# A decoder trunk in one kernel: other staging places, another queue and another order in the gate passes of layer A

## The chip, the cores and the metric

The kernel runs on one core of a Trainium2 chip. The metric is device time in microseconds (us) of one execution; a smaller number is better. Beside the times of whole executions there is one profiled execution, with a trace of every instruction. Engines are named as in the profile: PE multiplies matrices, PEld loads its stationary operand, DVE is the vector engine, ACT the scalar engine, POOL is GpSimd, and SP issues most of the data transfers. POOL issues transfers too, on a queue of its own. Each of these engines works its instructions off in the order in which they stand in its own program, and semaphores hold an instruction back until what it needs is there.

## What is computed

A trunk of two decoder layers over 512 tokens of width 2048, in float32. Layer A, in which the change lies, is sparse attention with a gate:

```
proj = x @ w_in
q, k, v, gate, iq, ik, iw = split(proj)          # 16 query heads, 4 key/value groups of 128
q, k = partial_rope(q), partial_rope(k)           # the first 32 of each head's 128 rows turn
iscore = sum_h relu(iq_h . ik) * iw_h * scale     # an index score for each query and key
idx = top_k(iscore, 128)                          # causal; 128 keys for each query
wts = softmax(q . k[idx] / sqrt(128))
o = wts @ v[idx]
h = (o * silu(gate)) @ w_o
x = layer_norm(alpha * x + h); x = x + (p @ w_p) * sigmoid(x @ w_g)
```

Layer B has the same frame around a stick-breaking attention. Every product is made of float32 operands that are split into two parts each, a high and a low one, and is the sum of three matmuls (high by high, high by low, low by high; lines 147 to 149).

## The kernel before

**Weights.** A weight tile comes from memory into a `raw` place (tiles `raw`, or a lent home, which the trace shows as `f` or `t`). ACT writes its high part (`wh` or `sh`), DVE then its low part (`wl` or `sl`); there are three buffers of each of the four names. So each weight costs one ACT and one DVE instruction, and two matmuls in three need it.

**Strassen in four passes.** Keys and values (columns of `w_in`), and then the gates, are computed with seven products in place of eight (m1 to m7). `gemm_quarters` runs a pass: for each of 8 steps along the contraction it takes one weight for each product of the pass and makes 2 x 3 matmuls of 512 columns with it. For the gates the first pass makes m2 and m4 from weights as they come, the second m1 and m7 (m7 from a difference of weights: one more DVE instruction a step), the third m6, m5 and m3 (from sums of weights: three more a step). The pass that follows the gates, called the chunk here, is `gemm_s` with `added_items`: the last quarter of the queries, all seven products at once with matmuls of 256 columns. Its weight sums for units 3 to 7 are prepared by transfers that add on arrival (lines 492 to 494: one on SP's queue, two on POOL's); those of units 0 to 2 by two more DVE instructions each.

**What sets the order.** PE's order is written by hand in the generators. Other work is put between PE's steps: `steps(gemm, n)` lets n PE steps (three matmuls each) be written, `pumped_at(gemm, when)` takes a piece of the queue `bg` at each step listed in `when`, and `paced(...)` pins an instruction to its place in the program. What isn't pinned is placed by a scheduler. On DVE and ACT all of this ends up in one row.

**The pieces in the queue.** `rounds` are the last rounds of the search for the 128 largest index scores: each is a MAX and a MATCH_REPLACE (a read of 8 largest values, and their removal), and the last piece is a mask of two instructions. `rounds[2:]` are two rounds and the mask.

**Keys.** The four key groups are complete before the gates' first pass. Their place `Kf` (the tile F[1], `f` in the trace) is needed for gate squares, so each group is turned (DVE, STREAM_TRANSPOSE in blocks of 32) into one of two halves of the tile `kx` (`stage`), and sent from there to memory (`turned_keys`, `kd` in the trace). The third and fourth group must wait until the first and second have been read out of `kx`. `key_back(g, b)` brings a quarter of a group back: for b = 0 the 32 rows that turn come into the packed tile `KP` (`rp` in the trace), and `key_turns` turns them there (a shuffle, two products, a sum); for b = 1, 2, 3 the others come straight into `Kf` later, in the chunk. Each is one DMA of 64 KB.

**Gate squares.** Inside the chunk, `turn_gate(g, t, rows)` applies SiLU to one half of a gate quarter (ACT), turns it (DVE) into a half of `kx` chosen by `stage(t)`, and `gates_out` sends it to memory (`heldg`). There are eight squares, and two places: the third must wait until the first has been read out, and so on. The gate quarters still have to be summed in between (`add_gates`, one DVE instruction each, with the tiles `u` and `t5` among the summands).

**Evictions at the end of a pass.** Results leave PSUM by ACT or DVE. Of the gates' m1, a copy goes to `u` (ACT) and a sum into c11 (DVE, `f<-f,m`), written behind the second pass; PE needs the banks of m1 again for m3, the third product of the third pass (line 1235: `m6, m5, m3 = pair(1, "m6"), pair(3, "m5"), pair(5, "m3")`, and m1, m7 are `pair(5)`, `pair(7)`).

Of the kernel before, what the change touches and what calls it, by code (L numbers as in the profile page):

```python
# [28 lines left out]
C_Q, C_K, C_V, C_G, C_IQ, C_IK = 0, 2048, 2560, 3072, 5120, 6144  # L29
# [22 lines left out]
def steps(gen, n):  # L52
    for _ in range(n):
        next(gen, None)
# [23 lines left out]
def trunk_kernel(  # L78
# [16 lines left out]
    nc = tc.nc  # L95
# [315 lines left out]
    bg = deque()  # L411

    def paced(fn, *args):
        was, pinned[0] = pinned[0], True
        fn(*args)
        pinned[0] = was
# [9 lines left out]
    def pumped_at(gen, when):  # L426
        for i, _ in enumerate(gen):
            if bg and i in when:
                one()
            yield  # L430
# [8 lines left out]
    def drain():  # L439
        while bg:  # L440
            one()
# [138 lines left out]
    def gemm_quarters(items, products):  # L580

        for k in range(NK // 2):
            for get, outs in products:
                pinned[0] = True
                w = next(items)
                pinned[0] = False
                h, l = get(k)
                for j, out in enumerate(outs):
                    s = slice(j * 128, (j + 1) * 128)
                    mm3(out, (h[:, s], l[:, s]), w, k == 0, k == NK // 2 - 1)  # L590
                    yield
# [268 lines left out]
    turned_keys = [dram.tile([128, 4, 128], F32, name=f"kd{g}") for g in range(4)]  # L860
# [42 lines left out]
    held_g = {g: dram.tile([4, 128, 4, 128], F32, name=f"heldg{g}") for g in (1, 2)}  # L903
# [6 lines left out]
    items = Ahead(all_items(), 2)  # L910
# [75 lines left out]
    gemm = first_pair(two)  # L986
    gemm = pumped_at(gemm, (*(46 + 5 * i // 2 for i in range(28)), *range(120, 128, 2)))
# [102 lines left out]
    gemm = pumped_at(both(), (*range(0, 32, 2), *range(34, 104, 3), *range(104, 128, 2)))  # L1090
# [14 lines left out]
    sp = pc_.enter_context(ss(name="spa", bufs=1, side="right"))  # L1105
    u, t3, t4, t5, kx = (sp.tile([128, 2, T], F32, name=n) for n in ("u", "t3", "t4", "t5", "kx"))
# [14 lines left out]
    def half(row, t):  # L1121
        return lambda k: (XH[k + row][:, t : t + H], XL[k + row][:, t : t + H])

    def summed(i):
        return lambda k: tuple(part[:, k] for part in CA[i])

    gemm = pumped(queries(2, (7, 0, 1, 2)), 3)
# [15 lines left out]
    rounds = [bg.pop() for _ in range(len(bg) - 2)][::-1]  # L1143
    for n, k in zip((0, 1, 2, 3, 5, 6, 8, 9), range(8)):
        bg.insert(n, lambda k=k: split(XH[k][:, H:T], XL[k][:, H:T], T1[1][k]))
    m2, m4 = pair(3, "m2"), pair(5, "m4")
# [8 lines left out]
    m1, m7 = pair(1, "m1"), pair(7, "m7")  # L1155
# [37 lines left out]
    def key_rows(g, rows=slice(0, 128)):  # L1193
        return Kf[rows, :, g * 128 : (g + 1) * 128]

    def stage(n):
        return kx[:, n % 2].rearrange("p (b n) -> p b n", b=4)

    def key_back(g, b):
        src = turned_keys[g].rearrange("(a j) b n -> b j a n", a=4)[b]  # L1200
        fetched = nc.sync.dma_start(key_rows(g, slice(32 * b, 32 * b + 32)) if b else KP[32 * g : 32 * g + 32], src)
        tc.keep_in_program_order(fetched)

    m2, m4 = pair(1, "m2"), pair(3, "m4")
    gemm = pumped_at(gemm_quarters(gates, ((half(8, 0), m2), (summed(2), m4))), (1, 5, 9, 13, 17))
    steps(gemm, 19)
    for g in range(4):
        paced(turn_blocks, stage(g), key_rows(g))
        steps(gemm, 3)
        nc.sync.dma_start(turned_keys[g], stage(g))  # L1210
    run(gemm)
    drain()
    c11, c12, c21, c22 = F[1][:, 0:2], F[3][:, 2:4], F[1][:, 2:4], F[3][:, 0:2]
# [2 lines left out]
    for j in range(2):  # L1216
        paced(lambda: act.activation(c21[:, j], m4[j], AF.Copy, scale=-1.0))
    m1, m7 = pair(5, "m1"), pair(7, "m7")
    bg.extend(rounds[2:])
    key_turns = turned_rows(KP, lambda g: key_rows(g, slice(0, 32)), by_place, by_token)  # L1220
    gemm = pumped_at(gemm_quarters(gates, ((half(0, 0), m1), (summed(1), m7))), range(1, 32, 4))
    steps(gemm, 11)
    for g in range(4):
        key_back(g, 0)
        steps(gemm, 1)
    steps(gemm, 4)
    bg.extend(key_turns[:3])
    run(gemm)
    drain()
# [8 lines left out]
    two = [flat[0][:, 4 * n : 4 * n + 4].rearrange("p a t -> p (a t)") for n in range(2)]  # L1238
    third, fourth = (t.rearrange("p a t -> p (a t)") for t in (t3, t4))
    places = [(two[0], two[1], third, fourth)[n % 4] for n in range(8)]  # L1240
    items = Ahead(added_items(w_in_a, (C_Q + 1536,), places, sp, range(3, 8)), 2)
    paced(items.prime)
    steps(gemm, 2)
    for j in range(2):
# [16 lines left out]

    turned_gates = deque()

    def turn_gate(g, t, rows):
        paced(act.activation, rows, rows, AF.Silu)
        paced(turn_blocks, stage(t), rows.rearrange("p (a n) -> p a n", a=4))
        turned_gates.append((g, t))

    def gates_out():
        g, t = turned_gates.popleft()  # L1270
        tc.keep_in_program_order(nc.sync.dma_start(held_g[g][t], stage(t)))

    steps(gemm, 3)
    turn_gate(1, 0, c11[:, 0])
# [21 lines left out]
    def some_back(n):  # L1296
        for _ in range(n):
            key_back(*backs.pop(0))
            steps(gemm, 2)

    some_back(3)
    add_gates(c12, t5)
    some_back(5)
    add_gates(c12, u)
    some_back(4)
    steps(gemm, 1)
    for g, t, rows in ((2, 2, c22[:, 0]), (2, 3, c22[:, 1]), (1, 2, c12[:, 0])):
        turn_gate(g, t, rows)
        steps(gemm, 7)
        gates_out()  # L1310
    nc.gpsimd.dma_start(F[0][:, 0:2], held_q[0][:, 0:2])
    turn_gate(1, 3, c12[:, 1])
# [1 line left out]
    gates_out()  # L1314
    run(gemm)
    drain()

    nc.gpsimd.dma_start(F[0][:, 2:4], held_q[0][:, 2:4])
    items = Ahead(rest_items(), 2).prime()
# [1269 lines left out]
```

## Time and profile before

| | |
|---|---|
| runs shown | 1815.38, 1813.75, 1807.22 us; median 1813.75 |
| profiled execution | 1807.65 us |
| its span, first to last instruction | 1805.4 us |
| PE busy | 1794.0 us of the span |
| DVE busy | 1534.2 us |
| ACT busy | 1055.1 us |
| POOL busy | 59.3 us |
| gates' first pass on PE | about 307 to 329 us from the span's start |
| gates' second pass | about 329 to 351 us |
| gates' third pass | about 351 to 386 us |
| the chunk | about 386 to 431 us |

A row of the timeline has the start and the duration in us, the engine, the line of the source, the operation, what it writes and reads, and how many like it were merged; in square brackets stands the time for which the engine was idle before it, and what ended that. `L118` is a helper through which every ACT and DVE instruction is recorded, so those are told apart by tiles. A waits row has the engine and line that waited, what ended the wait, the total, how often, and the longest.

### The profile page before, as it was taken

The numbers are of one execution on the slowest core, as the hardware profiler recorded it, in microseconds if no ns is written. First come the engines' busy times: TensorE is split into PE (matmuls) and PEld (weight loads), VectorE is DVE, ScalarE is ACT, GpSimd is POOL, SyncE is SP. The second block draws the span as 40 slices with busy tenths as digits, with TensorE's granted clock in tenths as the row PEclk, the third lists the DMA queues.
The fourth block names the chain that finished last, engine by engine and source line by source line (L and its number), as shares of the span: only waits on it lengthen the run. The fifth ranks groups of instructions, "written<-read, shape, count | busy, mean of one in ns | idle before, by whom it ended". The sixth has DMA issues, their size and how long they took to land. (4 is left out here: it accounts for less than half of the span.)

```text
span 1805.4 us, 26352 instructions
## 1 busy us (share of the span) xinstructions
PE 1794.0 (99%) x9191; PEld 1538.9 (85%) x9191; DVE 1534.2 (85%) x2958; ACT 1055.1 (58%) x1937; POOL 59.3 (3%) x113
## 2 busy tenths in 40 slices
PE   9999999999999999999999999999999999999999
PEld 9888888788888899888888888887788889988898
DVE  7888999898878899976568889978887889997997
ACT  4554355456676544575346554578888854557644
POOL 0001110011030000000000000001000000000000
PEclk9999999999999999999999999999999999999999
DMA  7524477766431344422438777736432244434344
GB/s 219 162 74 151 153 230 233 220 195 195 133 92 47 108 125 128 132 95 96 144 111 264 232 250 238 257 106 158 127 106 71 70 117 129 141 116 144 125 146 123
DMA packets 145780, 269.27 MB, mean 149 GB/s; under 512 B 13232, under 2 KB 57776, under 8 KB 144368
## 3 DMA queue, kind: packets, MB, share of 16 engines
q1 hardware_dynamic: 139728, 250.42, 44.8%
q0 software_dynamic: 5632, 16.78, 3.5%
q8 instruction: 72, 1.18, 0.3%
q14 instruction: 60, 0.49, 0.1%
q10 hardware_dynamic: 288, 0.39, 0.1%
HBM read 239.50 MB, written 23.07 MB: 145 GB/s over the span
## 5 line engine op out<-in xcount | busy, mean ns | idle before, releaser
L118 ACT ACTIVATE wh<-raw 128x512 fp32r<-128x512 f32 (+2 forms) x477 | 267.0, 561 | 333.9 <-PE g L148 121.1
L118 DVE TENSOR_TENSOR wl<-raw,wh 128x512 fp32r<-128x512 f32 (+2 forms) x476 | 286.2, 602 | 100.2 <-ACT wh L118 94.6
L147 PE MATMUL g<-xh,wh 128*128 128x512 f32 (+1 forms) x816 | 317.4, 389 | 0.0
L149 PE MATMUL g<-xh,wl 128*128 128x512 f32 (+1 forms) x816 | 314.9, 386 | 0.4 <-DVE wl L116 0.4
L148 PE MATMUL g<-xl,wh 128*128 128x512 f32 (+1 forms) x816 | 314.8, 386 | 0.0
L149 PEld LDWEIGHTS g<-xh,wl 128*128 128x128 f32 x816 | 153.3, 188 | 31.8 <-DVE wl L116 0.8
L147 PEld LDWEIGHTS g<-xh,wh 128*128 128x128 f32 x816 | 153.5, 188 | 29.6 <-ACT wk L116 0.3
L148 PEld LDWEIGHTS g<-xl,wh 128*128 128x128 f32 x816 | 153.5, 188 | 29.1
L118 ACT ACTIVATE sh<-f 128x512 fp32r<-128x512 f32 x116 | 72.5, 625 | 92.7 <-DVE f L118 80.9
L147 PE MATMUL o<-xh,wh 128*128 128x512 f32 x256 | 99.6, 389 | 0.0
L148 PE MATMUL o<-xl,wh 128*128 128x512 f32 x256 | 99.6, 389 | 0.0
L149 PE MATMUL o<-xh,wl 128*128 128x512 f32 x256 | 99.6, 389 | 0.0
L147 PE MATMUL m<-sh,xh 128*128 128x512 f32 x234 | 91.2, 390 | 2.6 <-DVE f L118 2.6
L148 PE MATMUL m<-sl,xh 128*128 128x512 f32 x234 | 91.2, 390 | 0.0
L149 PE MATMUL m<-sh,xl 128*128 128x512 f32 x234 | 91.1, 389 | 0.0
L118 DVE TENSOR_TENSOR sl<-f,sh 128x512 fp32r<-128x512 f32 x116 | 79.8, 688 | 12.1 <-ACT sh L118 11.9
L118 ACT ACTIVATE wh<-f 128x512 fp32r<-128x512 f32 x69 | 43.5, 630 | 60.2 <-DVE f L118 33.1
L147 PE MATMUL q<-xh,wh 128*128 128x512 f32 x192 | 74.9, 390 | 0.0
L148 PE MATMUL q<-xl,wh 128*128 128x512 f32 x192 | 74.9, 390 | 0.0
L149 PE MATMUL q<-xh,wl 128*128 128x512 f32 x192 | 74.9, 390 | 0.0
L118 DVE TENSOR_TENSOR xl<-f,xh 128x512 fp32r<-128x512 f32 (+1 forms) x102 | 57.7, 582 | 13.5 <-ACT f L118 12.0
L147 PE MATMUL m<-c,sh 128*128 128x256 f32 x240 | 67.9, 283 | 0.0
(502 smaller groups left out, 4794.5 us busy)
## 6 DMA issues: line engine op xcount, KB each, us to landing
raw<-w_in_a SPq DMA_DIRECT2D x95, 512.0 KB, 4.0
raw<-w_in_b SPq DMA_DIRECT2D x64, 512.0 KB, 4.0
raw<-w_ple_gate SPq DMA_DIRECT2D x44, 512.0 KB, 3.7
raw<-w_o_a SPq DMA_DIRECT2D x24, 512.0 KB, 4.3
raw<-w_o_b SPq DMA_DIRECT2D x24, 512.0 KB, 4.3
f<-w_in_a SPq DMA_DIRECT2D x22, 512.0 KB, 4.7
f<-w_in_b SPq DMA_DIRECT2D x16, 512.0 KB, 4.8
raw<-w_kv_b SPq DMA_DIRECT2D x16, 512.0 KB, 4.4
```

Of the source, the lines that this page charges most:

```text
L118: ins = method(*args, **kw)
L147: pe.matmul(out, a[0], b[0], start=start, stop=False)
L148: pe.matmul(out, a[0], b[1], start=False, stop=False)
L149: pe.matmul(out, a[1], b[0], start=False, stop=stop)
```

## The change

Five edits, all in layer A:

- `stage` has six places in place of two: the halves of `kx`, of `u` and of `t5`. The eight gate squares use 0, 1, 0, 1, 2, 3, 4, 5 in turn. The keys still use 0 and 1.
- `key_back(g, 0)`, the four fetches of the rows that turn, are issued by POOL's queue ahead of the second pass, and not by SP's inside it. The turning itself is put at steps 14, 18 and 22 of the second pass.
- The two search rounds and the mask stand in the gates' first pass, not in the second.
- The weight sums of the chunk's unit 7 are made by DVE, not by transfers (`range(3, 7)`).
- Of the twelve fetches of the other key rows, the six of groups 2 and 3 are issued behind the chunk. The sums and turns of gate squares at the chunk's end stand at other steps.

```diff
     def stage(n):
-        return kx[:, n % 2].rearrange("p (b n) -> p b n", b=4)
+        return (kx, u, t5)[n // 2][:, n % 2].rearrange("p (b n) -> p b n", b=4)
 
     def key_back(g, b):
         src = turned_keys[g].rearrange("(a j) b n -> b j a n", a=4)[b]
-        fetched = nc.sync.dma_start(key_rows(g, slice(32 * b, 32 * b + 32)) if b else KP[32 * g : 32 * g + 32], src)
-        tc.keep_in_program_order(fetched)
+        if b:
+            tc.keep_in_program_order(nc.sync.dma_start(key_rows(g, slice(32 * b, 32 * b + 32)), src))
+        else:
+            nc.gpsimd.dma_start(KP[32 * g : 32 * g + 32], src)
 
     m2, m4 = pair(1, "m2"), pair(3, "m4")
-    gemm = pumped_at(gemm_quarters(gates, ((half(8, 0), m2), (summed(2), m4))), (1, 5, 9, 13, 17))
+    gemm = pumped_at(gemm_quarters(gates, ((half(8, 0), m2), (summed(2), m4))), (1, 5, 9, 13, 17, 21, 25, 29))
+    bg.extend(rounds[2:])
     steps(gemm, 19)
...
     m1, m7 = pair(5, "m1"), pair(7, "m7")
-    bg.extend(rounds[2:])
     key_turns = turned_rows(KP, lambda g: key_rows(g, slice(0, 32)), by_place, by_token)
-    gemm = pumped_at(gemm_quarters(gates, ((half(0, 0), m1), (summed(1), m7))), range(1, 32, 4))
-    steps(gemm, 11)
+    gemm = pumped_at(gemm_quarters(gates, ((half(0, 0), m1), (summed(1), m7))), (14, 18, 22))
     for g in range(4):
         key_back(g, 0)
-        steps(gemm, 1)
-    steps(gemm, 4)
     bg.extend(key_turns[:3])
...
-    items = Ahead(added_items(w_in_a, (C_Q + 1536,), places, sp, range(3, 8)), 2)
+    items = Ahead(added_items(w_in_a, (C_Q + 1536,), places, sp, range(3, 7)), 2)
...
+    stages = deque((0, 1, 0, 1, 2, 3, 4, 5))
+
     def turn_gate(g, t, rows):
         paced(act.activation, rows, rows, AF.Silu)
-        paced(turn_blocks, stage(t), rows.rearrange("p (a n) -> p a n", a=4))
-        turned_gates.append((g, t))
+        at = stage(stages.popleft())
+        paced(turn_blocks, at, rows.rearrange("p (a n) -> p a n", a=4))
+        turned_gates.append((g, t, at))
...
     some_back(3)
     add_gates(c12, t5)
-    some_back(5)
+    some_back(3)
+    steps(gemm, 4)
     add_gates(c12, u)
-    some_back(4)
-    steps(gemm, 1)
+    steps(gemm, 5)
     for g, t, rows in ((2, 2, c22[:, 0]), (2, 3, c22[:, 1]), (1, 2, c12[:, 0])):
         turn_gate(g, t, rows)
-        steps(gemm, 7)
+        steps(gemm, 8)
         gates_out()
...
     run(gemm)
     drain()
+    for g, b in backs:
+        key_back(g, b)
```

PE's own order is the same instruction for instruction. What moves on DVE is shown at three places. In the rows below, `f_109`, `f_110` and `f_112` are the tiles F[0], F[1] and F[3]; `t_1684`, `t_1685` and `t_1686` are t3, t4 and t5; `am` and `wk` are the index scores and their working copy, and `m_` ahead of a number the eight largest or, where DVE adds to it, a product in PSUM.

The first place is DVE's row at the end of the gates' first pass, from the third turned key group on, in the kernel before:

```order
L118 STREAM_TRANSPOSE kx<-f_110 128x512
L118 TENSOR_TENSOR wl<-t_1684,wh 128x512
L118 STREAM_TRANSPOSE kx<-f_110 128x512
L118 TENSOR_TENSOR f_112<-t_1685 128x512
L118 TENSOR_TENSOR sl<-t_1685,sh 128x512
L118 TENSOR_TENSOR wl<-f_112,wh 128x512
L118 TENSOR_TENSOR f_112<-raw 128x512
L118 TENSOR_TENSOR sl<-raw,sh 128x512
L118 MAX m_2110<-wk 128x8
L118 MATCH_REPLACE wk<-m_2110,wk 128x512
```

The same stretch of DVE's row in the changed kernel:

```order
L118 STREAM_TRANSPOSE kx<-f_110 128x512
L118 MAX m_2110<-wk 128x8
L118 MATCH_REPLACE wk<-m_2110,wk 128x512
L118 TENSOR_TENSOR wl<-t_1684,wh 128x512
L118 STREAM_TRANSPOSE kx<-f_110 128x512
L118 TENSOR_TENSOR f_112<-t_1685 128x512
L118 TENSOR_TENSOR sl<-t_1685,sh 128x512
L118 TENSOR_TENSOR am_135<-wk,am_135 128x512
L118 TENSOR_SCALAR am_135<-am_135 128x512
L118 TENSOR_TENSOR wl<-f_112,wh 128x512
L118 TENSOR_TENSOR f_112<-raw 128x512
L118 TENSOR_TENSOR sl<-raw,sh 128x512
```

One round now stands behind the third turned group and the mask a little later; the other round stands ahead of this piece, between the first and the second turned group. In the kernel before, the two rounds and the mask begin where its piece ends.

The second place is DVE's row where the second pass goes over into the third, up to the sum into c11 (`f_110<-f_110,m`), in the kernel before:

```order
L118 TENSOR_TENSOR sw<-sw,Sq 128x512
L118 TENSOR_TENSOR wl<-f_112,wh 128x512
L118 TENSOR_TENSOR t_1684<-raw,f_109 128x512
L118 TENSOR_TENSOR t_1684<-t_1684,raw 128x512
L118 TENSOR_TENSOR f_112<-f_109,t_1684 128x512
L118 TENSOR_TENSOR sl<-kx,sh 128x512
L118 TENSOR_TENSOR rp<-rp,Cq 128x512
L118 TENSOR_TENSOR wl<-t_1684,wh 128x512
L118 TENSOR_TENSOR f_110<-f_110,m_3210 128x512
L118 TENSOR_TENSOR f_110<-f_110,m_3211 128x512
L118 TENSOR_TENSOR rp<-rp,sw 128x512
```

The same in the changed kernel:

```order
L118 TENSOR_TENSOR rp<-rp,Cq 128x512
L118 TENSOR_TENSOR f_112<-raw,f_109 128x512
L118 TENSOR_TENSOR rp<-rp,sw 128x512
L118 TENSOR_TENSOR kx<-f_112,raw 128x512
L118 TENSOR_TENSOR kx<-f_109,kx 128x512
L118 TENSOR_TENSOR sl<-kx,sh 128x512
L118 TENSOR_TENSOR wl<-f_112,wh 128x512
L118 TENSOR_TENSOR t_1684<-raw,f_109 128x512
L118 TENSOR_TENSOR t_1684<-t_1684,raw 128x512
L118 TENSOR_TENSOR f_112<-f_109,t_1684 128x512
L118 TENSOR_TENSOR sl<-kx,sh 128x512
L118 TENSOR_TENSOR wl<-t_1684,wh 128x512
```

The sum into c11 is the next row. The last two rope instructions now stand ahead of the sums of the third pass; before, two of the four stood among them, and the last behind the sum into c11.

The third place is DVE's row at the end of the chunk, from the first turned square of the last four on, in the kernel before:

```order
L118 STREAM_TRANSPOSE kx<-f_112 128x512
L118 TENSOR_TENSOR wl<-raw,wh 128x384
L118 TENSOR_TENSOR sl<-t_1684,sh 128x512
L118 STREAM_TRANSPOSE kx<-f_112 128x512
L118 TENSOR_TENSOR t_1685<-t_1685,raw 128x256 x2
L118 TENSOR_TENSOR wl<-raw,wh 128x384
L118 TENSOR_TENSOR sl<-t_1685,sh 128x512
L118 STREAM_TRANSPOSE kx<-f_112 128x512
L118 TENSOR_TENSOR wl<-raw,wh 128x384
L118 TENSOR_TENSOR sl<-t_1685,sh 128x512
L118 STREAM_TRANSPOSE kx<-f_112 128x512
```

From the second square of the last four on, in the changed kernel:

```order
L118 STREAM_TRANSPOSE u<-f_112 128x512
L118 TENSOR_TENSOR wl<-raw,wh 128x384
L118 TENSOR_TENSOR sl<-t_1684,sh 128x512
L118 TENSOR_TENSOR t_1685<-raw 128x256 x2
L118 STREAM_TRANSPOSE t_1686<-f_112 128x512
L118 TENSOR_TENSOR t_1685<-t_1685,raw 128x256 x2
L118 TENSOR_TENSOR wl<-raw,wh 128x384
L118 TENSOR_TENSOR sl<-t_1685,sh 128x512
L118 TENSOR_TENSOR wl<-raw,wh 128x384
L118 TENSOR_TENSOR sl<-t_1685,sh 128x512
L118 STREAM_TRANSPOSE t_1686<-f_112 128x512
```

The first three of these four squares stand a step earlier, the fourth stands where it stood; each goes to a place of its own. The pair `t_1685<-raw` is new: the sums of unit 7. On SP's queue the four `rp<-kd` and one add-on-arrival transfer are gone, and six of the `f_110<-kd` stand behind the last square; on POOL's queue the four `rp<-kd` stand ahead of the chunk's transfers, and two add-on-arrival transfers are gone.

More of the change, by code (lines that the diff above doesn't have):

```diff
@@ L1196, in stage @@
     def stage(n):
-        return kx[:, n % 2].rearrange("p (b n) -> p b n", b=4)
+        return (kx, u, t5)[n // 2][:, n % 2].rearrange("p (b n) -> p b n", b=4)
     def key_back(g, b):
         src = turned_keys[g].rearrange("(a j) b n -> b j a n", a=4)[b]
-        fetched = nc.sync.dma_start(key_rows(g, slice(32 * b, 32 * b + 32)) if b else KP[32 * g : 32 * g + 32], src)
-        tc.keep_in_program_order(fetched)
+        if b:
+            tc.keep_in_program_order(nc.sync.dma_start(key_rows(g, slice(32 * b, 32 * b + 32)), src))
+        else:
+            nc.gpsimd.dma_start(KP[32 * g : 32 * g + 32], src)
     m2, m4 = pair(1, "m2"), pair(3, "m4")
-    gemm = pumped_at(gemm_quarters(gates, ((half(8, 0), m2), (summed(2), m4))), (1, 5, 9, 13, 17))
+    gemm = pumped_at(gemm_quarters(gates, ((half(8, 0), m2), (summed(2), m4))), (1, 5, 9, 13, 17, 21, 25, 29))
+    bg.extend(rounds[2:])
     steps(gemm, 19)
     for g in range(4):
-        paced(turn_blocks, stage(g), key_rows(g))
+        paced(turn_blocks, stage(g % 2), key_rows(g))
         steps(gemm, 3)
-        nc.sync.dma_start(turned_keys[g], stage(g))
+        nc.sync.dma_start(turned_keys[g], stage(g % 2))
     run(gemm)
@@ L1262, in trunk_kernel @@
     turned_gates = deque()
+    stages = deque((0, 1, 0, 1, 2, 3, 4, 5))
     def turn_gate(g, t, rows):
         paced(act.activation, rows, rows, AF.Silu)
-        paced(turn_blocks, stage(t), rows.rearrange("p (a n) -> p a n", a=4))
-        turned_gates.append((g, t))
+        at = stage(stages.popleft())
+        paced(turn_blocks, at, rows.rearrange("p (a n) -> p a n", a=4))
+        turned_gates.append((g, t, at))
     def gates_out():
-        g, t = turned_gates.popleft()
-        tc.keep_in_program_order(nc.sync.dma_start(held_g[g][t], stage(t)))
+        g, t, at = turned_gates.popleft()
+        tc.keep_in_program_order(nc.sync.dma_start(held_g[g][t], at))
     steps(gemm, 3)
```

## The prediction

> **What bounds the kernel now.** I read the page's head first, then who PE waited for, then the timeline around each wait.
>
> ```profile
> span 1805.4 us, 26352 instructions
> PE 1794.0 (99%) x9191; PEld 1538.9 (85%) x9191; DVE 1534.2 (85%) x2958; ACT 1055.1 (58%) x1937; POOL 59.3 (3%) x113
> ```
>
> PE is busy for all but 11.4 us, some 4 of them ahead of its first product. Its order does not change, so the time can fall only by its waits, and by matmuls that run slowly behind one. The view of waits, for PE, gives the two that count:
>
> ```profile
> PE m L147 <- DVE f L118: 2.6, 1, 2.6
> PE m L149 <- DVE wl L118: 2.5, 1, 2.5
> ```
>
> The others are 0.8 us at the start and four of 0.2 to 0.4. The timeline puts the first wait at m3's first matmul in the gates' third pass:
>
> ```profile
> 353.15 0.39 PE L149 MATMUL m<-wh,xl 128*128 128x512 f32 x1
> 356.13 0.50 PE L147 MATMUL m<-sh,xh 128*128 128x512 f32 x1 [2.60 <-DVE f L118]
> 356.47 0.39 PE L148 MATMUL m<-sl,xh 128*128 128x512 f32 x1
> 356.70 0.40 PE L149 MATMUL m<-sh,xl 128*128 128x512 f32 x1
> ```
>
> Matmuls start 0.23 us apart (the last two rows), so this one was due at 353.38: **wait 1 costs 2.75 us**. DVE's row at that time:
>
> ```profile
> 354.20 0.68 DVE L118 TENSOR_TENSOR rp<-rp,Cq 128x512 f32<-128x512 f32 x1
> 354.80 0.69 DVE L118 TENSOR_TENSOR wl<-t,wh 128x512 fp32r<-128x512 f32 x1
> 355.40 1.28 DVE L118 TENSOR_TENSOR f<-f,m 128x512 f32<-128x512 f32 x2
> ```
>
> PE waits for `f<-f,m`, the sum into c11 that frees m1's first bank. DVE was not waiting but late. It had fallen behind since the turned keys:
>
> ```profile
> 326.56 0.71 DVE L118 STREAM_TRANSPOSE kx<-f 128x512 f32<-128x512 f32 x1 [2.69 <-DMA kd<-kx]
> ...
> 332.28 0.69 DVE L118 TENSOR_TENSOR sl<-raw,sh 128x512 fp32r<-128x512 f32 x1 [1.17 <-ACT sh L118]
> 332.89 0.69 DVE L118 MAX8 m<-wk 128x8 f32<-128x512 f32 x1
> ...
> 334.28 0.68 DVE L118 TENSOR_TENSOR wl<-f,wh 128x512 fp32r<-128x512 f32 x1
> ...
> 339.28 0.69 DVE L118 TENSOR_TENSOR am<-wk,am 128x512 f32<-128x512 f32 x1
> ...
> 340.35 0.69 DVE L118 TENSOR_TENSOR wl<-t,wh 128x512 fp32r<-128x512 f32 x1
> ...
> 342.41 0.69 DVE L118 TENSOR_TENSOR wl<-f,wh 128x512 fp32r<-128x512 f32 x1 [0.18 <-ACT wh L118]
> ```
>
> From 326.56 to 355.40 DVE idles 1.7 us. A search round takes 334.28 - 332.89 = 1.39 us of it, the mask 340.35 - 339.28 = 1.07.
>
> The second wait is at the chunk's end:
>
> ```profile
> 424.43 0.28 PE L147 MATMUL m<-xh,wh 128*128 128x256 f32 x1
> 424.55 0.28 PE L148 MATMUL m<-xl,wh 128*128 128x256 f32 x1
> 427.31 0.58 PE L149 MATMUL m<-xh,wl 128*128 128x256 f32 x1 [2.48 <-DVE wl L118]
> ...
> 430.98 0.40 PE L147 MATMUL g<-xh,wh 128*128 128x512 f32 x1
> ```
>
> Twenty starts lie from 424.55 to the first `g`. At the 0.12 us of the first two rows they would take 2.40 us; they took 6.43. **Wait 2 costs 4.03 us**: 2.64 as the gap (427.31 less 424.67), 1.39 because the matmuls behind it run slowly. The view of windows has the granted clock there, the last number but two, 0.60:
>
> ```profile
> 427.30:431.00 3.70, 3.69 (x20) 3.69 (x21) 3.60 (x6) 1.73 (x3) 0.00 (x0) 0.60 0.86 275
> ```
>
> DVE's row shows why:
>
> ```profile
> 426.11 0.71 DVE L118 STREAM_TRANSPOSE kx<-f 128x512 f32<-128x512 f32 x1 [5.13 <-DMA heldg<-kx]
> 426.74 0.52 DVE L118 TENSOR_TENSOR wl<-raw,wh 128x384 fp32r<-128x384 f32 x1
> ```
>
> A gate square could not be turned until another had left `kx`; the weight that PE needed stood behind it.
>
> **The change, part by part.** *Six places.* The last four squares go to places that nothing is being read out of, so the 5.13 us are gone. DVE gets the sums of unit 7 instead; the like for unit 2:
>
> ```profile
> 392.81 0.75 DVE L118 TENSOR_TENSOR t<-raw 128x256 f32<-128x256 f32 x2
> ```
>
> So the weight comes 5.13 - 0.75 = 4.38 us earlier, where 2.64 were missing: 1.7 us to spare, and wait 2 goes whole, with the slow matmuls: **-4.0 us**. Next in line is the first `g` weight, which DVE writes behind the last square: 4.4 us earlier as well, for a PE that comes 4.0 earlier.
>
> Of this, 1.39 us hang on the clock. The matmuls behind wait 1, which is as long, start 0.23 us apart, as those ahead of it; those behind wait 2 ran at 0.60. The trace has a drop behind one gap in two, so it is not certain that every execution pays it there, or doesn't pay it behind wait 1 as well: 1.4 us either way, kept for the range. [...]
>
> *Rounds in the first pass.* DVE meets the third key group's wait later by one round, 1.39 us, which its 2.69 us of idleness hides. The second round and the mask, 2.46 us, now follow that wait. Up to the low part at 332.28, DVE's own work is 4.4 us from 326.56 (5.72 less 1.35 of idleness); with 2.46 it ends near 333.4 - 333.6, where the ACT evictions that it waited for before are past. It then writes `wl<-f` at about 334.2, as before (334.28), and from there saves one round and the mask: 2.46 us.
>
> *Rope rows.* The four rope instructions take 0.6 us each. Three stood ahead of `f<-f,m`, now all four: +0.6. Of DVE's short waits for ACT's high part, which a round or a rope instruction used to cover, three come back, of 0 to 0.25 us each. So `f<-f,m` starts 2.46 + 0.1 - 0.6 - (0 to 0.75) = 1.2 to 1.95 us earlier; I take 1.5, the middle. Wait 1 shrinks to 1.25 us: **-1.5 us**. Bounds: nothing, if a later key transfer eats it, and 2.75, if DVE's 1.7 us of idleness goes too. Beyond it DVE is 2.1 us early (the fourth rope instruction is gone from behind) and PE 1.5, so the third pass has no less cover than before.
>
> The rows must be in `rp` when DVE comes to the shuffle, now behind the low part at 342.41: 343.0 - 2.2 = 340.8. The trace has no `rp<-kd` on POOL; its nearest row is that of the 64 KB transfers of turned rows on POOL, by its line:
>
> ```profile
> L1062 POOL DMA_DIRECT2D f<-rp x20: 498/498/857, 155.7 to 491.6; - x20
> ...
> DMA to landing us min/median/max: 1.8/1.9/7.5
> ```
>
> Ahead of them come the four key writes `kd<-kx` on SP, by theirs:
>
> ```profile
> DMA to landing us min/median/max: 2.4/4.0/5.5
> ```
>
> The fourth key group is turned behind the third (326.56), a round and two instructions of 0.6 us: its write goes out at about 329.9 and lands at 332.3 to 335.4; the last fetch is issued then and lands 1.8 to 7.5 us later: 334.1 to 342.9. I take 337 (the medians are 334 and 1.9, and the load here is nearer to that of the longer rows): 3.8 us ahead of its use, cost nothing. At the far end the shuffle waits 2.1 us and wait 1 is back whole, and 0.6 more.
>
> [...]
>
> *Six fetches behind the chunk.* The last square is turned two weight parts behind 426.74 and written at about 428.5; six fetches later it is 431.5, and the last lands by 439.2 at the longest:
>
> ```profile
> L1201 SPq DMA_DIRECT2D f<-kd x12: 303/470/1526, 405.1 to 417.7; - x12
> ...
> DMA to landing us min/median/max: 3.2/6.7/7.7
> ```
>
> ```profile
> 443.89 0.62 ACT L118 ACTIVATE kh<-f 128x512 fp32r<-128x512 f32 x1
> ```
>
> The third key group is split at 443.89, and all of this moves together: 4.7 us of cover. Nothing.
>
> Sum: -1.5 - 4.0 = -5.5 us. The profiled execution took 1807.65 us, its span 1805.4 and 2.25 around it: **1802.1 us**.
>
> **Level.** Of four executions of before, 1807.22 and 1807.65 lie together, 1813.75 and 1815.38 higher. The median shown, 1813.75, is 6.1 above the one that I can read. Both waits end, directly or in the end, with a transfer's landing, and in this trace such landings spread by 3 us (`kd`) and more; a later one lengthens them one for one. So part of the upper level may be these waits. But no trace shows it.
>
> **Rivals.** (a) *The upper level is something else and stays*: 1813.75 - 5.5 = 1808.2. For it: nothing ties it to these waits. (b) *The slack is eaten in the first pass*: the low part at 332.28 is used by PE at 334.56, and would now be ready at about 334.3. If the first key write lands a microsecond later, PE waits there, and wait 1 keeps its length: -4.0 or somewhat less, 1803.6 to 1806. For it: DVE is busy throughout; against: PE's wait there and at c11 are the same lateness, paid once. (c) *Slower: the rope rows come late by POOL.* DVE stops at the shuffle with every later weight behind it. From 340.8 on, each microsecond lengthens wait 1; from 340.8 + 5.5 = 346.3 on it costs more than both savings, and 1807.65 is exceeded; 355 would give 1816. [...] Against: the 0.5 us of `f<-rp`, issued twenty times beside a DVE that is busy for 85% of the span. (d) *The places don't help*, because a square still waits for a transfer: the order of DVE's row, with four targets, excludes it.
>
> **How the numbers follow.** Forecast at the lower level, up to 1803.5: 0.42. Rival (a), 1805 to 1811: 0.38. Rival (b), 1803.6 to 1806: 0.15, half of it under 1804.7. Rival (c): 0.05, put down to slower, since its price has no upper end. A measurement of this kernel tells about 0.5% from no change, 9 us: faster is below 1804.7, slower above 1822.8. Faster 0.42 + 0.07 = 0.49, same 0.38 + 0.08 = 0.46, slower 0.05. Bounds of the unknown costs: both waits gone whole is 1807.65 - 6.8 = 1800.9, less the clock's 1.4 and some spread, 1798.5; upwards to (a) and its spread, 1811.
>
> **What would show it.** In the changed trace: no DVE wait for `heldg`, no PE wait at the chunk's end, the clock 1.00 there; a wait of about 1.25 us on `f<-f,m` at 353 (if gone, I undervalued the second edit; if 2.7, rival (b)); the shuffle without a wait for `rp<-kd`. A PE wait elsewhere in 330 to 460 us, or a DVE wait for `rp`, makes the prediction wrong.

## The result

| | before | changed |
|---|---|---|
| executions, measured side by side | 15 | 15 |
| lowest to highest, us | 1805.44 to 1817.07 | 1799.28 to 1807.57 |
| median, us | 1812.79 | 1800.52 |
| profiled execution, us | 1807.65 | 1800.91 |
| its span, us | 1805.4 | 1799.0 |

The ratio of the changed kernel to the one before is 0.9939, with an interval of 0.9926 to 0.9953: 0.6% faster. Thirteen of the fifteen executions of the changed kernel lie at 1799.3 to 1802.1; two stand apart, at 1807.2 and 1807.6.

The head of the profile after, and its whole view of PE's waits (engine, line, what ended the wait; total, times, longest):

```profile
span 1799.0 us, 26345 instructions
PE 1792.4 (100%) x9191; PEld 1537.6 (85%) x9191; DVE 1535.1 (85%) x2960; ACT 1052.9 (59%) x1937; POOL 59.5 (3%) x115
```

```profile
PE m L147 <- DVE f L118: 1.1, 1, 1.1
PE spun L167 <- PEq L2584: 0.8, 1, 0.8
```

Of wait 1, part is left; of wait 2, nothing; and the four small waits of before are gone as well. The timeline of PE around what is left of wait 1:

```profile
353.62 0.39 PE L149 MATMUL m<-wh,xl 128*128 128x512 f32 x1
355.15 0.50 PE L147 MATMUL m<-sh,xh 128*128 128x512 f32 x1 [1.14 <-DVE f L118]
355.48 0.39 PE L148 MATMUL m<-sl,xh 128*128 128x512 f32 x1
```

The matmul was due at 353.85 and costs 1.30 us, not 2.75. DVE's timeline shows why:

```profile
326.75 0.71 DVE L118 STREAM_TRANSPOSE kx<-f 128x512 f32<-128x512 f32 x1 [1.02 <-DMA kd<-kx]
...
333.86 0.69 DVE L118 TENSOR_TENSOR sl<-raw,sh 128x512 fp32r<-128x512 f32 x1 [0.38 <-ACT sh L118]
334.47 0.68 DVE L118 TENSOR_TENSOR wl<-f,wh 128x512 fp32r<-128x512 f32 x1
...
341.31 0.73 DVE L118 STREAM_SHUFFLE sw<-rp 128x512 f32<-128x512 f32 x1
...
354.42 1.28 DVE L118 TENSOR_TENSOR f<-f,m 128x512 f32<-128x512 f32 x2
```

The wait for the first turned key group has shrunk from 2.69 to 1.02 us, the wait for ACT's high part from 1.17 to 0.38; the shuffle has no wait at all; and the sum into c11 starts at 354.42 instead of 355.40, in a run that was 0.47 us later at its start.

At the end of the chunk, the last of the eight squares in DVE's timeline, and the window of PE there (length, then busy time of PE, PEld, DVE, ACT and POOL, the granted clock, the share of DMA, GB/s):

```profile
422.04 0.70 DVE L118 STREAM_TRANSPOSE t<-f 128x512 f32<-128x512 f32 x1
```

```profile
421.00:425.00 4.00, 4.00 (x36) 4.00 (x35) 3.32 (x7) 2.52 (x6) 0.00 (x0) 1.00 0.79 260
```

No square waits for `heldg`, PE is busy throughout, and the clock is 1.00 where it was 0.60.

PE runs the same 9191 matmuls in the same order in both kernels, so the start of each can be set against its twin's, and the difference read along the span. It is +0.47 us ahead of wait 1 (a later start), -0.98 behind it, -1.17 ahead of wait 2, -5.20 behind it, -5.58 behind 455 us, -5.40 behind 1083 us, and then falls again, to -6.66 at 1280 us, far behind everything that the change touches. That last step is in layer B.

### The profile page after: what moved, and what is told of

The parts are those of the page before. It is cut to its first block, busy times and chain, and to the rows that moved or that the text cites. A ratio compares the mean times of both kernels' runs of the same rounds, so it can differ in the third digit from the quotient of the medians.

```text
span 1799.0 us, 26345 instructions
## 1 busy us (share of the span) xinstructions
PE 1792.4 (100%) x9191; PEld 1537.6 (85%) x9191; DVE 1535.1 (85%) x2960; ACT 1052.9 (59%) x1937; POOL 59.5 (3%) x115
## 4 chain that ended last, share of the span: by engine, by line
PE 98%; DMA 1%; DVE 1%; ACT 0%; issue 0%
PE m L147 12%; PE m L149 12%; PE m L148 12%; PE g L147 10%; PE g L148 10%; PE g L149 10%; PE o L148 4%; PE o L149 4%; PE o L147 4%; PE q L148 2%; PE q L147 2%; PE q L149 2%; PE iq L149 1%; PE iq L148 1%; PE iq L147 1%; PE z L2356 1%
```

## The experiments

Theory at the outset (W): the spread of before's executions comes from waits 1 and 2, so that it goes with them. Rival (O): it comes from somewhere else. Eleven kernels were run, the two themselves among them, in three groups. The kernel before ran beside each group and had a median of 1813.17, 1812.1 and 1811.2 us in the three; every ratio below is to that of its own group.

### The kernel before, once more

> The kernel before, unchanged, to see an execution of its upper level (over 1810 us). Theory W (the spread is made by the two waits): if the profiled execution is of the upper level, wait 2 (the transposed square that waits for a square's write, 5.13 us of DVE and 4.03 us of PE in the known trace) or wait 1 (2.75 us) is longer by what the execution is over 1807.65 us, for instance 6 us at 1814. Rival O (the spread comes from elsewhere): both waits have their known lengths within 1 us, and the extra time is spread over the span or lies ahead of 300 us or behind 460 us. The times: median 1810 to 1815 us, from 1805 to 1817.

Measured: 1812.2 us (1807.58 to 1816.50, 11 executions). The profiled one took 1811.78 us. Its PE waits:

```profile
PE g L149 <- DVE wl L116: 3.9, 1, 3.9
PE m L149 <- DVE wl L118: 3.0, 1, 3.0
PE m L147 <- DVE f L118: 1.3, 1, 1.3
```

Wait 1 is shorter here than in the first profile and wait 2 a little longer. With the slow matmuls behind it they cost 6.0 us together, against 6.8 in the first profile, so they don't make this execution slow. A third wait does. PE's timeline, and the window behind it:

```profile
1259.14 0.39 PE L148 MATMUL g<-xl,wh 128*128 128x512 f32 x1
1263.44 0.80 PE L149 MATMUL g<-xh,wl 128*128 128x512 f32 x1 [3.90 <-DVE wl L116]
1264.03 0.63 PE L147 MATMUL g<-xh,wh 128*128 128x512 f32 x1
1264.46 0.63 PE L148 MATMUL g<-xl,wh 128*128 128x512 f32 x1
```

```profile
1263.40:1266.80 3.40, 3.36 (x9) 2.70 (x10) 2.43 (x5) 2.45 (x4) 0.00 (x0) 0.56 0.29 73
```

The matmul was due 0.23 us behind the one before it, so the gap costs 4.06 us, and the ones behind it start 0.43 us apart instead of 0.23, at a granted clock of 0.56. For this execution theory W falls: **wait 3 is in layer B**, some 830 us behind the change.

What PE waits for is a weight's low part, and DVE is held up by a transfer (DVE's timeline):

```profile
1258.49 0.71 DVE L116 STREAM_TRANSPOSE wu<-f 128x512 f32<-128x512 f32 x1 [6.85 <-DMA f<-wu]
...
1262.70 0.68 DVE L116 TENSOR_TENSOR wl<-raw,wh 128x512 fp32r<-128x512 f32 x1
```

The transfer is the last of five that add on arrival (`add_queries`): layer B's query blocks, also made by Strassen, are summed by POOL's queue, each one waiting for the one before. Its timeline in this execution and in the changed kernel's (in brackets POOL's idle time ahead of each; where an ACT is named, that was long done, and where `E<-kd` is, the issue comes 0.52 us behind the landing of the add before, as in the other executions):

```profile
1220.22 0.94 POOL L2279 DMA_DIRECT2D f<-wu  x1 [0.53 <-issue]
1227.46 0.87 POOL L2279 DMA_DIRECT2D f<-f  x1 [6.30 <-DMA f<-wu]
1235.79 0.86 POOL L2279 DMA_DIRECT2D f<-f  x1 [7.46 <-ACT xh L116]
1243.83 0.86 POOL L2279 DMA_DIRECT2D f<-wt  x1 [7.18 <-DMA E<-kd]
1251.62 0.87 POOL L2279 DMA_DIRECT2D f<-wu  x1 [6.93 <-DMA f<-wt]
```

```profile
1215.01 0.94 POOL L2283 DMA_DIRECT2D f<-wu  x1 [0.53 <-issue]
1221.89 0.87 POOL L2283 DMA_DIRECT2D f<-f  x1 [5.94 <-DMA f<-wu]
1228.42 0.86 POOL L2283 DMA_DIRECT2D f<-f  x1 [5.65 <-ACT c L116]
1233.79 0.86 POOL L2283 DMA_DIRECT2D f<-wt  x1 [4.51 <-ACT wk L116]
1242.19 0.86 POOL L2283 DMA_DIRECT2D f<-wu  x1 [7.53 <-DMA f<-wt]
```

From the first issue to the last landing this **chain** takes 38.26 us here (1258.47 less 1220.22), and 31.70 in the changed kernel (1246.71 less 1215.01). About 34.2 us are hidden behind PE: 38.26 less the gap's 4.06.

### The six places alone, and the changed kernel with two

The first kernel is the one before with the six places and nothing else:

```diff
-        return kx[:, n % 2].rearrange("p (b n) -> p b n", b=4)
+        return (kx, u, t5)[n // 2][:, n % 2].rearrange("p (b n) -> p b n", b=4)
...
+    stages = deque((0, 1, 0, 1, 2, 3, 4, 5))
```

> The kernel before with six staging places alone. W: wait 2 is gone and the upper level with it; median 1802 to 1804.5 us (after's 1800.5 and wait 1 in its full length of 2.75 us, 1.5 more than after), ratio 0.994 to 0.996, most executions within 3 us of each other. O: wait 2's 4.0 us are gone and the spread stays: median 1808.8 us, ratio 0.998, executions from 1801 to 1813.

Measured: 1804.75 us (1802.77 to 1806.92, 5 executions), ratio 0.9957 (0.9945 to 0.9969). Wait 2 is gone: the shift against before goes from -0.34 us ahead of it to -4.37 behind.

The median lies 8.4 us below that of before in the same group, twice what wait 2 costs in the traces, and no execution took over 1807. That is nearer to what theory W expected than to theory O's 1808.8 us with the spread left. The one profile, of the fastest of the five, has a chain of 34.87 us; that the longer chain became rarer by the places alone, and why it should, is not shown.

The second is the changed kernel with two places:

```diff
-    stages = deque((0, 1, 0, 1, 2, 3, 4, 5))
+    stages = deque((0, 1, 0, 1, 0, 1, 0, 1))
```

> The changed kernel with two staging places for the squares, all else changed. W: wait 2 is back, DVE waits for heldg in the profile, PE loses 2.5 us or more there, and the spread is back: median 1806 to 1811 us, ratio 0.996 to 0.999. O: wait 2 is back at about 4 us and the executions lie together: median 1804.5 us, within 3 us of each other, ratio 0.9955.

Measured: 1802.95 us (1800.80 to 1812.28, 6 executions), ratio 0.9951 (0.9936 to 0.9967). In the profile, which is that of the 1812.28, the wait is back at an earlier square. DVE, and PE:

```profile
421.21 0.71 DVE L118 STREAM_TRANSPOSE kx<-f 128x512 f32<-128x512 f32 x1 [2.77 <-DMA heldg<-kx]
```

```profile
421.08 0.28 PE L148 MATMUL m<-xl,wh 128*128 128x256 f32 x1
423.21 0.39 PE L149 MATMUL m<-xh,wl 128*128 128x256 f32 x1 [1.85 <-DVE wl L118]
```

The gap costs 2.01 us, and the matmuls behind it, at a granted clock of 0.67 from 423 to 427 us, nearly as much: across the gap and them, the shift against the changed kernel grows by 3.9 us. The two runs put the price of the places at 3.9 to 4.0 us where the wait occurs. Not every execution need have it: one with two places took 1800.80. Four of the six lie at 1800.8 to 1803.5 and two at 1810.3 and 1812.3, which neither theory had. The rest of this profile's lateness is wait 3 again, with a chain of 38.46 us.

### The rounds and the mask back in the second pass

```diff
     gemm = pumped_at(gemm_quarters(gates, ((half(8, 0), m2), (summed(2), m4))), (1, 5, 9, 13, 17, 21, 25, 29))
-    bg.extend(rounds[2:])
...
+    bg.extend(rounds[2:])
-    gemm = pumped_at(gemm_quarters(gates, ((half(0, 0), m1), (summed(1), m7))), (14, 18, 22))
+    gemm = pumped_at(gemm_quarters(gates, ((half(0, 0), m1), (summed(1), m7))), (1, 5, 9, 14, 18, 22))
```

> The changed kernel with the two search rounds and the mask back in the gates' second pass. W and O alike by the prediction's ledger: f<-f,m starts 1.86 us later (two rounds and the mask less the idle time that one round filled), less the waits for ACT that the rounds cover again (0 to 0.75), so wait 1 is 1.3 + 1.1 to 1.9 = 2.4 to 3.2 us in the profile and the median is 1801.6 to 1802.4 us, ratio 0.994 to 0.9955. A rival to the ledger: the rounds are hidden either way and wait 1 was shortened by the rope rows; then wait 1 stays at 1.3 us and the median at 1800.5.

Measured: 1802.8 us (1801.48 to 1804.0, 5 executions), ratio 0.9945 (0.9934 to 0.9957). PE's timeline at the change from the second to the third pass:

```profile
351.44 0.39 PE L149 MATMUL m<-wh,ca 128*128 128x512 f32 x1
352.80 0.50 PE L147 MATMUL m<-sh,ca 128*128 128x512 f32 x1 [0.98 <-ACT sh L118]
353.53 0.50 PE L148 MATMUL m<-sl,ca 128*128 128x512 f32 x1 [0.22 <-DVE sl L118]
...
355.91 0.39 PE L149 MATMUL m<-wh,xl 128*128 128x512 f32 x1
357.98 0.50 PE L147 MATMUL m<-sh,xh 128*128 128x512 f32 x1 [1.69 <-DVE f L118]
```

The three gaps cost 1.14, 0.50 and 1.85 us, 3.49 in all, where the changed kernel has one of 1.30. So in these two profiles the rounds' new place is worth 2.2 us beside the rope rows on POOL; the time is a little above the expected 1802.4. Part of DVE's lateness comes out as a wait for the third pass's weights, ahead of the sum into c11.

### The chain of layer B begun sooner (before), and later (changed)

The first is the kernel before:

```diff
-    beside_turn(0, 4, add_queries)
+    beside_turn(0, 3, add_queries)
```

> The kernel before, with the five adding transfers of layer B's query sums begun one turn sooner (about 5.3 us). Theory C: in the six profiles so far the time from the issue of the first to the landing of the fifth was 34.8, 38.3, 34.9, 38.5, 31.6 and 31.7 us, and TensorE's wait near 1259 us was about that minus 34.2; this chain, not the two waits of layer A, is what parts the runs of before. Then the wait near 1259 us is gone, and the runs lie at 1806 to 1809 us with no second level (median about 1807.3, 5 to 6 us below before in the same call). Rival O: the spread comes from elsewhere and the wait near 1259 us moves to another weight: 1812 to 1814.

Measured: 1805.94 us, ratio 0.9971 (0.9957 to 0.9985); 11 executions at 1804.19 to 1811.02, and one at 1931.17 far apart, which is in neither number. Wait 3 is gone from the profile, where the chain ends at 1251.01 us. Of the 31 executions of before beside it 16 took over 1812, here none of the 11. But three of them lie at 1809.4 to 1811.0, above what was expected, so the chain isn't all of the spread.

The second is the changed kernel:

```diff
-    beside_turn(0, 4, add_queries)
+    beside_turn(0, 5, add_queries)
```

> The changed kernel with the chain begun one turn later (5 to 6 us). Theory C: the adds take 31.6 to 38.5 us, 34.2 us of them were hidden, so 5 to 6 us less cover gives a wait near 1259 us of 3 to 10 us and, with it, the lower clock behind it: 1804 to 1811 us, no run at 1800. Rival (the wait near 1259 us has another cause and the chain is hidden): 1800 to 1802 as the changed kernel.

Measured: 1806.63 us (1805.88 to 1808.83, 10 executions), ratio 0.9975 (0.9965 to 0.9985): 6.3 us above the changed kernel in the same group. PE's timeline:

```profile
1252.91 0.39 PE L148 MATMUL g<-xl,wh 128*128 128x512 f32 x1
1257.19 0.79 PE L149 MATMUL g<-xh,wl 128*128 128x512 f32 x1 [3.89 <-DVE wl L116]
1257.78 0.63 PE L147 MATMUL g<-xh,wh 128*128 128x512 f32 x1
```

The gap is made to order, 4.05 us and the slow matmuls behind it, with a chain of only 31.34 us. Both runs bear out that the chain's end against PE's need sets wait 3.

### What sets the chain's length

The profiles with the chain at its usual place, in us. The second column is when POOL's issue of the second add ended, from the chain's start; SP's issue of a weight fetch (`raw<-w_in_b`, 512 KB) ends 7.94 to 7.99 us after that start in all of them. The last is what PE's gap near 1259 us cost. Where there is a gap, chain less gap is 34.2 us in each of the five rows.

| kernel | second add issued by | it landed after | chain | gap |
|---|---|---|---|---|
| changed, again (below) | 7.71 | 5.68 | 31.22 | none |
| changed, rounds in second pass | 7.74 | 5.72 | 31.62 | none |
| changed | 7.75 | 5.71 | 31.70 | none |
| changed, banks swapped (below) | 7.81 | 5.82 | 31.92 | none |
| changed, two places | 7.98 | 8.24 | 38.46 | 4.28 |
| before, again | 8.11 | 7.82 | 38.26 | 4.06 |
| before, six places | 8.12 | 8.23 | 34.87 | 0.69 |
| before | 8.16 | 8.54 | 34.80 | 0.56 |
| changed, rope rows by SP (below) | 8.36 | 7.82 | 38.46 | 4.22 |
| before, two transfers more (below) | 8.39 | 7.90 | 34.13 | none |

Where the second add is on its way 0.13 us or more before the fetch, it lands 5.7 to 5.8 us after its issue and the chain takes 31 to 32 us. Where it comes behind, it takes 7.8 to 8.5 and the chain 34 to 38.5. Which of the two issues ends first is called the race below. That it does it is read from ten profiles, not tried by itself.

A second race follows at the fourth add, and it parts the chains of 34 us from those of 38. Another weight fetch meets it, whose issue ends 24.4 to 24.5 us after the chain's start in the six profiles with a late second add. In three of them (before, six places, two transfers more) the fourth add's issue ended 0.11 to 0.29 us ahead of the fetch's; this add took 5.7 us and the fifth 4.8 to 5.1. In the other three (before again, two places, rope rows by SP) it ended 0.06 to 0.15 us behind; this add took 7.2 to 7.5 us, and the fifth, behind one fetch more, 6.9 to 7.1. In the first profile of before the two issues are these rows of POOL and SP, with ends at 1244.77 and 1244.88:

```profile
1243.91 0.86 POOL L2279 DMA_DIRECT2D f<-wt  x1 [6.25 <-ACT wh L116]
```

```profile
1244.49 0.39 SPq L231 DMA_DIRECT2D raw<-w_in_b  x1
```

In before again POOL's (shown above) ends at 1244.69, and SP's at 1244.63:

```profile
1244.24 0.39 SPq L231 DMA_DIRECT2D raw<-w_in_b  x1
```

So before's two profiles both lose the first race, and the second, won by 0.11 us in the one and lost by 0.06 us in the other, goes with chains of 34.80 and 38.26 us. This too is read, not tried.

Why the changed kernel's add comes sooner is half answered. Its first add lands 6.6 us after its issue, as before (6.7), but the second follows the landing by 0.29 us, in before by 0.58. The transfers of POOL take turns on eight semaphores (numbers 111 to 118 in the traces of both kernels), and the change gives POOL two transfers more, 94 against 92, which puts the first add on 112 and not on 118. The next kernel gives before two more, by other means:

```diff
     tick = px.tile([128, 8], F32, name="tick")
+    spare = px.tile([128, 16], F32, name="spare")
+    for n in range(2):
+        pool.dma_start(spare[:, n * 8 : (n + 1) * 8], ident[:, 0:8])
```

> The kernel before, with two tiny transfers more on GpSimd's queue ahead of the chain (4 KB each into a tile that nothing reads), so that each adding transfer sits on the same one of GpSimd's eight transfer semaphores as in the changed kernel. Theory R: that place, not the staging places, decides how soon the second add follows the first (0.29 us after its landing as in the changed kernel, 0.57 to 0.59 us in before), and so whether it runs ahead of the weight fetch that is issued 7.58 us after the chain began (5.7 us) or beside it (7.8 to 8.5 us). Then the chain is 31 to 33 us here in most runs and the median is 1807 to 1808.5. Rival: the place is without effect, the gaps are those of before, and the median is 1812 to 1814.

Measured: 1809.55 us (1807.69 to 1816.42, 12 executions), ratio 0.9993 (0.9979 to 1.0008), which is not told apart from before. The gaps between the adds did become the changed kernel's (0.30, 0.82, 0.52 and 0.28 us). But in the profiled execution the first add took 7.22 us instead of 6.7, the race was lost all the same, and the chain took 34.13 us, not 31 to 33. So with two transfers more ahead of the chain the second add follows after 0.30 us and not after 0.58; that this is what wins the race isn't shown. Only one of the twelve executions took over 1812 us, where 16 of 31 did in before, so the longest chain may have become rarer; no profile tells.

### The rope rows by SP

```diff
-        if b:
-            tc.keep_in_program_order(nc.sync.dma_start(key_rows(g, slice(32 * b, 32 * b + 32)), src))
-        else:
-            nc.gpsimd.dma_start(KP[32 * g : 32 * g + 32], src)
+        fetched = nc.sync.dma_start(key_rows(g, slice(32 * b, 32 * b + 32)) if b else KP[32 * g : 32 * g + 32], src)
+        tc.keep_in_program_order(fetched)
...
-    gemm = pumped_at(gemm_quarters(gates, ((half(0, 0), m1), (summed(1), m7))), (14, 18, 22))
+    gemm = pumped_at(gemm_quarters(gates, ((half(0, 0), m1), (summed(1), m7))), (15, 18, 22))
+    steps(gemm, 11)
     for g in range(4):
         key_back(g, 0)
+        steps(gemm, 1)
```

> The changed kernel, with the four rope rows fetched by SP inside the pass as before, all else as changed. Theory of the prediction (rope rows by GpSimd cost nothing and bring nothing by themselves): first and second pass within 0.5 us of the changed kernel's. What it can do in layer B: GpSimd has four transfers fewer, so the chain sits on other semaphores. If theory R holds, the gaps between the adds differ from the changed kernel's 0.29, 0.82, 0.51 and 0.29 us, and the time follows the chain: 1800 to 1801.5 if its second add still goes ahead of the weight fetch, 1803 to 1807 if not.

Measured: 1804.92 us (1803.23 to 1811.85, 12 executions), ratio 0.9970 (0.9956 to 0.9985). The expectation of nothing was wrong. SP's timeline, then DVE's:

```profile
336.61 0.80 SPq L1201 DMA_DIRECT2D rp<-kd  x2
338.04 0.35 SPq L210 DMA_DIRECT2D raw<-w_in_a  x1
338.44 0.91 SPq L1201 DMA_DIRECT2D rp<-kd  x2
```

```profile
344.63 0.01 DVE L118 LOAD_MASK_SELECT sw<-rp  x1 [3.67 <-DMA rp<-kd]
```

On SP's queue the rows go out from 336.61 us on, two behind a weight fetch at 335.97 and two behind another at 338.04, and land by 344.50; the shuffle, freed of the rounds ahead of it, waits 3.67 us. PE is 3.36 us behind the changed kernel past wait 1, more than the 2.2 us that the rounds' new place is worth. So the rounds' move pays here only with the rope rows coming earlier too: that is what POOL's queue is for.

Of theory R the times bear out the second half: the second add goes out behind the fetch, and the chain takes 38.46 us. The gaps between the adds are 0.29, 0.52, 0.62 and 0.29 us, so the first did not change with the place on the semaphores; the race was lost because the first add took 7.19 us.

### The changed kernel again, and two versions of it

> The changed kernel again, to stand beside the next two in the same call. Theory C (chain): its second add is issued ahead of the weight fetch in most executions (chain of 31.6 to 31.9 us in the profiles of the changed kernel and of the two that share its GpSimd queue and were fast), so most runs lie at 1799 to 1802 us, and the few in which the add comes behind the fetch at 1806 to 1808. Median 1800 to 1801.

Measured: 1800.37 us, ratio 0.9949 (0.9929 to 0.9968); five executions at 1799.45 to 1801.95, one at 1807.83. In the first version the sum's products trade their pairs of banks, and c22's copy is written first:

```diff
-    m1, m7 = pair(5, "m1"), pair(7, "m7")
+    m1, m7 = pair(7, "m1"), pair(5, "m7")
...
+    for j in range(2):
+        paced(act.activation, c22[:, j], m7[j], AF.Copy)
     for j in range(2):
         paced(act.activation, u[:, j], m1[j], AF.Copy)
         paced(dve.tensor_tensor, c11[:, j], c11[:, j], m1[j], ALU.add)
-    for j in range(2):
-        paced(act.activation, c22[:, j], m7[j], AF.Copy)
```

> The changed kernel, with the sum's two products in each other's pair of banks (m1 on 7, m7 on 5) and c22's copy written ahead of the sum, so that the third pass's first matmul needs the pair that is freed first. Theory: the wait of 1.30 us that is left at 354 us goes, and the pair freed later is needed one product later and not waited for: 1799.2 us, 1.3 us below the changed kernel's 1800.5. Rival: the wait moves to the other pair and nothing is won: 1800 to 1802.

Measured: 1800.91 us (1799.68 to 1807.45, 8 executions), ratio 0.9949 (0.9931 to 0.9968). PE's timeline, where the changed kernel waits 1.30 us:

```profile
353.43 0.39 PE L149 MATMUL m<-wh,xl 128*128 128x512 f32 x1
353.65 0.39 PE L147 MATMUL m<-sh,xh 128*128 128x512 f32 x1
```

The wait is gone from the trace, whose span of 1797.8 us is 1.2 us shorter than the changed kernel's. The times don't show it: the ratio to before is that of the changed kernel again, and two of the eight executions stand apart at 1807.4. The second version takes the swapped banks and the chain begun one turn sooner, both edits as above.

> The changed kernel with both cures: the sum's products in each other's banks (its profile had no wait left at 354 us, 1.5 us won there), and the chain of layer B begun one turn sooner. Theory C: no run at 1806 to 1808 any more, all at 1798.5 to 1801, median 1799.5, which beats the changed kernel by about 1 us. Rival: the chain begun sooner meets other fetches and nothing is won: median 1800.5 to 1802, outliers as before.

Measured: 1800.13 us (1799.17 to 1800.94, 5 executions), ratio 0.9940 (0.9924 to 0.9955). No execution stands apart, but in all only three in 21 of the changed kernel do (1807.2 to 1807.8), so five can't show that they are gone. In its profile a wait of 1.10 us for a weight's low part has come back at 359 us, twenty matmuls behind the old place: In this execution DVE is as late as before, and the swap only moved the matmul that meets it. No version was shown to beat the changed kernel.

## Why the prediction was right, and where not

- **Six places, -4.0 us.** Right in cause and size: -4.03 in the shift between the two profiles, -4.03 with the places alone, 3.9 lost with two. The gap behind `heldg` was there in all five profiles with two places.
- **Its 1.39 us of slow matmuls** were paid behind wait 2 in before's first profile, in its repeat and in two variants, so counting them was right. What was kept open, a drop behind wait 1 as well, happened in one: with two transfers more, the same gap as in before's first profile is followed by matmuls 0.43 us apart.
- **Wait 1, -1.5 us.** Right: -1.45, from 2.75 to 1.30 (forecast 1.25). On the way, the low part came at 333.86 (forecast 333.4 to 333.6), `wl<-f` at 334.47 (334.2). But the size was luck of the execution: before's repeat has 1.43, and the changed kernel's repeat 0.87, so that pair differs by 0.6.
- **Rope rows, nothing.** Right as a sum, since the shuffle didn't wait. The four landed by 336.48 us (forecast 337):

```profile
L1204 POOL DMA_DIRECT2D rp<-kd x4: 548/552/561, 327.0 to 333.0; - x4
```

  The four issues took 0.55 to 0.56 us each, with DVE busy for 2.11 of their 2.21 us, so the lateness of rival (c) doesn't show here. But the edit isn't an idle one: without it 3.36 us are lost.
- **Six fetches, nothing.** Right as far as the trace goes: no wait in their place. Neither this edit nor the sums of unit 7 was tried alone; with the places alone wait 2 was gone without them.
- **The sum.** Between the profiled executions it came to -6.74 us, not -5.5. What is missing is the step of 1.2 us near 1260 us: wait 3 in its shortest form. (The other differences, +0.47 at the start, -0.35 at 455 us and some smaller ones, happen to cancel.) The step that failed is in the first part, where "four of 0.2 to 0.4" were put aside. One of those was the gap of 0.56 us at 1259 us that the chain's 34.80 us leave uncovered, and a second of 0.32 follows it at 1262; neither is in the changed kernel. They marked a stretch with no slack left.
- **Level.** The second step that failed. "So part of the upper level may be these waits" isn't borne out by the profiles: in the upper one of before the two waits cost no more than in the lower one. What the upper one loses it loses behind the chain, which costs nothing up to 34.2 us of length; at 38.3 to 38.5 us the gap and the slow matmuls behind it come to 5.5 to 6.6 us in three profiles. That the changed kernel lies at the lower level came true for another reason than those weighed, which was luck: in both of its profiles the chain is the short one. The 8.4 us of the places alone are not accounted for by this.
- **Rival (a)**, 1808.2 us: its premise was right, since nothing tied the upper level to waits 1 and 2, but it took for granted that a level which has another cause stays. It may be what stays in three of 21 executions of the changed kernel, at 1807.2 to 1807.8, near what (a) has; none of the three was profiled, but two relatives of the kernel whose profiles show the race lost have the gap of 4.2 to 4.3 us at wait 3.

Of the 12.3 us between the medians, then, about half is what the change was worked out for. The repeats of the two kernels, profiled at 1811.78 and 1800.21 us, show it matmul by matmul: the changed one is 5.9 us ahead where wait 3 comes (0.3 of it from the start of the span) and 11.5 us ahead behind it. With the chain begun sooner on both sides the ratios to before are 0.9971 and 0.9940; the difference, 0.0031, is 5.6 us, give or take 4 (the second has the swapped banks as well, which no time shows to matter). The rest goes with the races in layer B, which the change tips by some tenths of a microsecond.

What is left open: why the first add lands after 6.6 us in some executions and after 7.2 in others; how often each kernel wins which race, since only a profile tells; why the places alone brought 8.4 us; and what else spreads before's executions with the chain begun sooner (1804 to 1811 us). For the last, wait 1, which cost from 1.2 to 4.4 us in the five profiles with before's first two passes, slow matmuls included, is the candidate.

## What to carry to other kernels

A row of small waits, of some tenths each, on an engine that is otherwise full can mark a stretch whose cover is just used up: follow it back before putting it aside, since a slower execution may pay there in full, as before's repeat did. Where the executions of a kernel spread by more than the gain that is looked for, profile a second one and compare matmul by matmul before the spread is put down to the waits at hand. A chain of transfers that wait for each other wants to begin as early as its inputs allow (begun one turn later, it cost the changed kernel 6.3 us); whether one of them is issued some tenths of a microsecond ahead of another large transfer or behind it went with 2 to 3 us here, and a change far ahead can tip that.

## What the runs showed of the hardware

The granted clock did not follow from a gap's length alone. Start to start, the gap of 2.76 us at wait 2 of before was followed by a stretch at 0.50, from 426.86 to 430.27 us, and one of 2.13 us (two places) by a mean of 0.67 from 423 to 427 us. Wait 1 of before, 2.98 us, was followed by 1.00 from 356.1 to 359.5 us, while 3.02 us at the same place in another kernel (two transfers more) was followed by 0.57 from 357.5 to 361.5 us. Behind gaps of nearly the same length at wait 3, the clock was 0.56 from 1263.4 to 1266.8 us in one profile (before again, 4.30 us; its matmuls start 0.23 us apart again from 1266.50 on), and 0.50 from 1257.0 to 1262.5 us in the other (chain begun later, 4.28 us).

How a gap lies in time differs as well. The stretch at 0.50 in before's first profile lasts 3.413 us. It begins 423.25 us behind the trace's first record of the clock, which is 124 times that length, and 1375.57 us, 403 times, pass from its end to the next change; in the changed kernel the only change comes 1792.00 us behind the first record, 525 times. Counted off in such lengths from these changes, the gap of wait 1 lies across a boundary: by the modelled ends of its matmuls PE was idle for 1.64 us from 351.77 to 355.18 us and for 0.96 us in the next length, both at 1.00. Wait 2 puts 2.03 us of idleness into one length, 423.45 to 426.86 us, and the one behind it is that at 0.50. What is left of wait 1 in the changed kernel puts 1.14 us into one, 353.26 to 356.67 us, and the clock stays at 1.00. That this is what decides is not shown: there is one such drop in these two profiles.

Two transfers of 512 KB whose issues end 0.2 us apart, the second add and the weight fetch, did not share evenly. With the add ahead it landed after 5.71 us and the fetch after 6.17 (the changed kernel); with the fetch ahead it took 4.70 and the add 8.54 (before). Issues that end 0.04 us apart had no such winner: in the changed kernel with two places the add took 8.24 us and the fetch 7.95.
